# Strassen products over twelve instead of eight k-tiles, with most of the weight sums made by accumulating DMAs

## The chip, the cores and the metric

The kernel runs on one core of a Trainium2 chip. The metric is the device time of one execution in microseconds, the median of several runs. A core has TensorE for matrix products, VectorE (DVE) and ScalarE (ACT) for elementwise work, GpSimd (POOL), SyncE (SP), whose queue here issues the loads, and 16 DMA engines that move data between HBM and the on-chip memory SBUF. TensorE writes its sums into eight PSUM banks.

## The reference

One decoder layer on 256 tokens of width 2048, all in float32:

```python
x = layer_norm(ALPHA * x + 0.5 * swiglu(x, ffn1_w_in[i], ffn1_w_out[i]), ln_g[i, 0], ln_b[i, 0])
z = x @ mix_w_in[i]
...
x = layer_norm(ALPHA * x + merged @ mix_w_out[i], ln_g[i, 1], ln_b[i, 1])
x = layer_norm(ALPHA * x + 0.5 * swiglu(x, ffn2_w_in[i], ffn2_w_out[i]), ln_g[i, 2], ln_b[i, 2])
ple = jax.nn.sigmoid(x @ ple_w_gate[i]) * (p[i] @ ple_w_proj[i])
x = layer_norm(ALPHA * x + ple, ln_g[i, 3], ln_b[i, 3])
```

`swiglu(x, w_in, w_out)` splits `x @ w_in` into halves a and u, each 5504 columns wide, and returns `(silu(a) * u) @ w_out`. The two feed-forward blocks hold most of the arithmetic, and the change is in their first product, `x @ w_in`. The input p is 256 wide and used only in the last product.

## The kernel before

**Three passes for one product.** Every operand is kept as a pair: h, its value rounded to the fast format fp32r, and l, the rest. A product is three matmuls, h x h, h x l and l x h (lines 962 to 964, in `passes`). The 128 x 128 block of tokens is the stationary operand, 512 columns of a weight are the moving one. There are two row blocks of tokens, t = 0 and 1, and a depth of 2048 is 16 k-tiles of 128.

**How a weight comes in.** Weights are handled in elements of two k-tiles x 512 columns, 512 KB. SP loads an element into a raw tile (`weight_dma`, line 868), ScalarE casts it to h (`weight_cast`, line 897), VectorE subtracts to get l (`weight_split`, line 908). The pairs h and l lie in a ring of six ("main", `NMAIN`), with some more in a few regions (`EXTRA`). `feed` runs after each consumed element and issues loads, casts and splits as far as buffers allow; `plan` is the list of all elements in the order in which TensorE uses them, and casts and splits follow it. Instructions of one engine run in the order that this gives.

**Chunks of a feed-forward block.** The 5504 columns of a and of u are cut into 11 chunks of up to 512. Chunks 0 and 1 are plain (`Unit`, one for a and one for u); chunks 2 to 10 are each a `Quad`, which treats the 2 row blocks and the 2 column blocks (a and u) together. After a chunk mostly two output products (`out_unit`) follow, which multiply an earlier chunk pair's result with `w_out`, eight k-tiles deep.

**Strassen in a Quad.** For four k-tiles (two "lo", two "hi"), the four column-block and depth-block parts of the weight are the tiles k11, k12, k21 and k22. Winograd's form of Strassen's method makes seven products instead of eight, into the banks p1 to p7: three elements of loaded tiles (11, 22, 21) and four sums of them (t1 to t4). The sums are made in place: t1 is k11 + k12 in k11's buffer, t3 is k12 + k22 in k12's, t2 adds k22 to k11's buffer, t4 adds k21 to it. Line 891, in `weight_cast`, is that sum on VectorE. The token side has its own sums s1 to s4, made once per block by `sums` from transposed plain copies of x. Two steps cover k-tiles 0 to 7. The other eight are ordinary elements a0, a1 (column block a, used for both row blocks) and u0, u1 (column block u); the Strassen form wants row block 0's u product as the difference d of the row blocks. In each step the order is 11 u0 t1 u1 22 t3 a0 t2 a1 21 t4. An element makes 6 passes, an a or u element 12. At the end of the second step, `after` combines the banks into the four results, applies silu and the product, and `turn` transposes the result three ticks later. A tick is one group of six passes; `defer` runs work a number of ticks later.

**Buffers.** Loaded Strassen tiles lie in a ring of five (`NSRAW`, tag `sraw`), shared with the plain copies of x until `sums` is through at tick 11 of its region; other raw tiles in a ring of four (`NRAW`). `may_load` lets a ring load when a buffer's last reader has been issued.

**The operand p.** `small_loads`, at the start of the program, loads p; `place` transposes it and makes its pair in tiles `ph` and `pl` of the pool `low`, which stay until the last stage.

Of the kernel before, what the change touches and what calls it, by code (L numbers as in the profile page):

```python
# [10 lines left out]
F32 = mybir.dt.float32  # L11
# [6 lines left out]
P = 128  # L18
D = 2048
S = 256  # L20
NT = 2
# [9 lines left out]
LONG = (12, 4)  # L31
EXTRA = {"lead1": 3, "ffn1": 0, "tail1": 4, "hgrn": 0, "merge": 0, "lead2": 3, "ffn2": 0, "tail2": 4, "ple": 1}
NSRAW = 5
# [33 lines left out]
class Quad:  # L67
# [10 lines left out]

    def __init__(self, stat, w, cols, width, after):
        self.stat, self.w, self.cols, self.width, self.after = stat, w, cols, width, after  # L80
        self.els = []
        for s in range(2):
            lo, hi = (2 * s, 2 * s + 1), (4 + 2 * s, 5 + 2 * s)
            n0, n1 = (8 + 4 * s, 9 + 4 * s), (10 + 4 * s, 11 + 4 * s)
            k11, k12, k21, k22 = ((self, s, n) for n in ("11", "12", "21", "22"))
            step = {
                "11": dict(src=k11, use=[("p1", 0, lo)]),
                "t1": dict(src=k11, add=k12, use=[("p5", "s1", lo)]),
                "22": dict(src=k22, use=[("p3", "s4", lo)]),
                "t3": dict(src=k12, add=k22, use=[("p7", "s3", lo)], free=[k12]),  # L90
                "t2": dict(src=k11, add=k22, use=[("p6", "s2", lo)], drop=[k22]),
                "21": dict(src=k21, use=[("p2", 0, hi)]),
                "t4": dict(src=k11, add=k21, use=[("p4", 1, hi)], drop=[k21], free=[k11]),
            }
            for n, ks in (("a0", n0), ("a1", n1)):
                step[n] = dict(load=[(ks, 0)], use=[("p2", 0, ks), ("p4", 1, ks)])
            for n, ks in (("u0", n0), ("u1", n1)):
                step[n] = dict(load=[(ks, 1)], use=[("p3", "d", ks), ("p5", 1, ks)])
            step["11"]["sums"] = [(k12, lo, 1), (k22, hi, 1), (k21, hi, 0), (k11, lo, 0)]
            order = "11 u0 t1 u1 22 t3 a0 t2 a1 21 t4".split()  # L100
            for n in order:
                self.els.append(dict(step[n], name=n, step=s))
# [3 lines left out]
def hybrid_layer(ctx: ExitStack, tc: tile.TileContext, x, p, ln_g, ln_b, ffn1_w_in, ffn1_w_out, mix_w_in,  # L106
# [24 lines left out]
    def open_region(kind):  # L131
# [6 lines left out]
        if kind.startswith("lead"):  # L138
            region["high"] = reopen("hctx", kind + "h", "right")
            held.update(sraw=0, freed=0)  # L140
# [135 lines left out]
    def high(name):  # L276
        held["sraw"] += 1
        return region["high"].tile([P, KG, CC], F32, tag="sraw", name=name, bufs=NSRAW)

    def plain_tile(t, c):  # L280

        if c % 2 == 0:
            plain[t, c // 2] = high("yT")
        return plain[t, c // 2][:, c % 2, :]

    def difference(a, b, o):
        nc.vector.tensor_tensor(out=o, in0=a, in1=b, op=ALU.subtract)

    def sums(stat):
        x1, x2, d = plain[0, 0], plain[1, 0], high("s3")  # L290
        x11, x12, x21, x22, s3 = x1[:, 0, :], x1[:, 1, :], x2[:, 0, :], x2[:, 1, :], d[:, 0, :]
        s1, s2, s4 = x21, x11, x12

        def made(key, g, src):
            halves(stat, key, g, src, 4, "s")

        def third():
            difference(x11, x21, s3)
            made("s3", 0, s3)

        def first():
            difference(x21, x22, s1)
            made("s1", 0, s1)

        def second():
            difference(s1, x11, s2)
            made("s2", 0, s2)

        def fourth():
            nc.vector.tensor_tensor(out=s4, in0=x12, in1=s2, op=ALU.add)  # L310
            made("s4", 0, s4)

        def delta(c):
            a = plain[0, 1][:, c % 2, :]
            difference(a, plain[1, 1][:, c % 2, :], a)
            made("d", c, a)
            if c == 3:
                held["freed"] += 5

        for i, fn in enumerate((third, first, second, fourth, lambda: delta(2), lambda: delta(3))):  # L320
            defer(1 + 2 * i, fn)
# [85 lines left out]
    def ffn(name, xs, w_in, w_out, ln_i, nxt):  # L407
# [7 lines left out]
        def in_units(ch, g, ci):  # L415
            c0 = starts[ch]
            w = starts[ch + 1] - c0
            if ch > 1:
# [8 lines left out]
                def after(el, ps):  # L427
                    if el["step"] == 0:
                        return
                    if el["name"] == "11":  # L430
                        made["c11"] = work("h")
                        nc.scalar.copy(made["c11"], ps["p1"])
                    elif el["name"] == "22":
                        made["c12"] = work("silu")
                        nc.scalar.copy(made["c12"], ps["p3"])
                        both(made["c12"], made["c12"], ps["p5"], ALU.add)
                    elif el["name"] == "t2":
                        made["e"], made["c22"] = work("silu"), work("h")
                        e = made["e"]
                        both(e, made["c11"], ps["p6"], ALU.add)  # L440
                        both(made["c12"], made["c12"], e, ALU.subtract)
                        both(e, e, ps["p7"], ALU.add)
                        both(made["c22"], ps["p5"], e, ALU.subtract)
                    elif el["name"] == "21":
                        h = made["c11"]
                        both(h, h, ps["p2"], ALU.add)
                        nc.scalar.activation(h, h, AF.Silu)
                        both(h, h, made["c12"], ALU.mult)
                        turn(g, 0, ci, h, CC)
                    elif el["name"] == "t4":  # L450
                        e = made["e"]
                        both(e, e, ps["p4"], ALU.add)
                        nc.scalar.activation(e, e, AF.Silu)
                        both(e, e, made["c22"], ALU.mult)
                        turn(g, 1, ci, e, CC)

                units.append(Quad(xs, w_in, (c0, DFF + c0), CC, after))
# [44 lines left out]
        units.append(("tail" + name, lambda: None))  # L502
# [14 lines left out]
    def small_loads():  # L517
# [6 lines left out]
        pin = [st.tile([P, CC], F32, tag="h", name="pin", bufs=3) for t in range(NT)]  # L524
        for t in range(NT):
            nc.sync.dma_start(pin[t][:, :256], p[0, 0, t * P : (t + 1) * P, :])

        def place():
            tp = ptile("t", "tp")
            nc.tensor.transpose(tp[:, :96], gb, ident[:96, :96])  # L530
            nc.vector.tensor_copy(gbT, tp[:, :96])
            for t in range(NT):
                tp = transposed(pin[t], 2)
                ph = low.tile([P, 2, P], F32R, tag=f"ph{t}", name="ph")
                pl = low.tile([P, 2, P], F32R, tag=f"pl{t}", name="pl")
                hf = ph.rearrange("p a b -> p (a b)")
                nc.scalar.copy(hf, tp[:, :256])
                nc.vector.tensor_tensor(out=pl.rearrange("p a b -> p (a b)"), in0=tp[:, :256],
                                        in1=hf.bitcast(F32), op=ALU.subtract)
                pst.parts[t, 0] = (ph, pl)  # L540

        defer(8, place)

# [255 lines left out]
    pst = Stat()  # L799
# [33 lines left out]
    loads = {"raw": deque(), "sraw": deque()}  # L833
    for u in units:
# [3 lines left out]
        if isinstance(u, Quad):  # L838
            for el in u.els:
                for key, ks, n in el.get("sums", ()):  # L840
                    loads["sraw"].append((key, kind, u.w, ks[0] * P, 2, u.cols[n], u.width))
                if "load" in el:
                    (ks, n), = el["load"]
                    el["src"] = len(plan)
                    el["free"] = [len(plan)]
                    loads["raw"].append((len(plan), kind, u.w, ks[0] * P, 2, u.cols[n], u.width))
                plan.append(dict(el, n=2, w=u.width, where="main"))
            continue
# [8 lines left out]
    used = {"raw": 0, "sraw": 0}  # L857
    room = dict(EXTRA, main=NMAIN)

    def weight_dma(ring="raw"):  # L860
# [4 lines left out]
        else:  # L865
            raw = high("sraw")
# [4 lines left out]
    def may_load(ring):  # L871
# [4 lines left out]
        return loads[ring][0][1] == region["kind"] and 5 <= held["freed"] and held["sraw"] - held["freed"] < NSRAW  # L876

    def drop(keys):
        for key in keys:
# [3 lines left out]
            else:  # L883
                held["freed"] += 1

    def weight_cast():
# [3 lines left out]
        if "add" in el:  # L890
            nc.vector.tensor_tensor(out=raw[:, :n, :w], in0=raw[:, :n, :w], in1=raws[el["add"]][:, :n, :w], op=ALU.add)  # L891
            drop(el.get("drop", ()))
# [19 lines left out]
    def castable():  # L912
# [135 lines left out]
```

## Time and profile before

| | us |
|---|---|
| median of three runs | 2227.79 (2227.02 to 2231.14) |
| the profiled execution | 2228.56 |
| its span, first to last instruction | 2226.7 |

In the profile, "busy" is the time in which an engine executed something; matmuls overlap, so TensorE's busy share says that it was never without one, not how fast it was. L963 is line 963. "bank<-wl,xh" is what is written from what is read, by the program's names. The feed-forward blocks lie at about 20 to 710 us and 1430 to 2130 us of the span.

### The profile page before, as it was taken

To read this page: it belongs to the slowest core of one execution; us is meant where nothing else is said; L and a number is where in the kernel's file an instruction comes from. 1 tells how busy PE (TensorE), PEld (TensorE's weight loads), DVE (VectorE), ACT (ScalarE), POOL (GpSimd) and SP (SyncE) were. 2 spreads that over 40 slices of the span, in tenths; PEclk is the share of its full clock that TensorE was granted. 3 is DMA by queue.
4 is the path that set the end of the run, shared out by engine and by line. 5 is a ranking of instruction groups with operands and counts; after the bars stand their busy time and mean duration, and the time that the engine had idled before them with its cause. 6 is when DMAs were issued, how large, how long until landed. Compare 5 with 4: busy or idle time off the path is not lost.

```text
span 2226.7 us, 26935 instructions
## 1 busy us (share of the span) xinstructions
PE 2203.0 (99%) x10110; PEld 1837.0 (82%) x10110; DVE 1685.6 (76%) x1952; ACT 1127.8 (51%) x1324; POOL 10.0 (0%) x32
## 2 busy tenths in 40 slices
PE   9999999999999999999999999999999999999997
PEld 7988888888887888888888888798888888888876
DVE  6788888888885678557555875769888888888668
ACT  5555555555555534434444443645555555555463
POOL 1000000000000000000000000000000000000000
PEclk9999999999999999999999999999999999999999
DMA  7666676566653665554555665567666556666564
GB/s 255 215 204 194 198 217 202 183 192 190 207 194 128 194 200 172 174 167 152 189 190 189 199 194 192 181 200 226 209 214 197 181 185 214 200 191 192 172 218 151
DMA packets 225334, 429.98 MB, mean 193 GB/s; under 512 B 13740, under 2 KB 22452, under 8 KB 225204
## 3 DMA queue, kind: packets, MB, share of 16 engines
q1 hardware_dynamic: 225204, 428.27, 60.6%
q8 instruction: 79, 1.29, 0.2%
q14 instruction: 51, 0.42, 0.1%
HBM read 426.12 MB, written 2.10 MB: 192 GB/s over the span
## 4 chain that ended last, share of the span: by engine, by line
PE 92%; DVE 4%; DMA 2%; ACT 1%; issue 1%; SPq 0%; DVEq 0%; ACTq 0%
PE bank L962 30%; PE bank L964 29%; PE bank L963 29%; DVE wl L908 2%; PE bank L243 2%; PE bank L600 1%; DVE sraw L891 1%; DMA raw<-in_ffn_w_in_dram 1%; ACT wh L897 0%; DMA sraw<-in_ffn_w_in_dram 0%; DMA gb<-in_ln_g_dram 0%; DMA x<-in_x_dram 0%; DMA raw<-in_ffn_w_out_dram 0%; DVE x L400 0%; DVE x L401 0%
## 5 line engine op out<-in xcount | busy, mean ns | idle before, releaser
L908 DVE TENSOR_TENSOR wl<-raw,wh 128x1024 fp32r<-128x1024 f32 (+2 forms) x660 | 788.6, 1203 | 262.8 <-ACT wh L897 245.4
L897 ACT CAST wh<-raw 128x1024 fp32r<-128x1024 f32 (+2 forms) x660 | 680.4, 1035 | 581.5 <-PE bank L964 410.1
L964 PE MATMUL bank<-wh,xl 128*128 128x512 f32 (+1 forms) x1736 | 670.9, 387 | 0.7 <-DVE xl L254 0.7
L963 PE MATMUL bank<-wl,xh 128*128 128x512 f32 (+1 forms) x1736 | 671.0, 387 | 0.0
L962 PE MATMUL bank<-wh,xh 128*128 128x512 f32 (+1 forms) x1736 | 669.6, 388 | 1.3 <-ACT xh L253 0.9
L897 ACT CAST wh<-sraw 128x1024 fp32r<-128x1024 f32 x252 | 262.5, 1050 | 273.1 <-PE bank L964 120.3
L908 DVE TENSOR_TENSOR wl<-sraw,wh 128x1024 fp32r<-128x1024 f32 x252 | 306.1, 1223 | 102.5 <-ACT wh L897 98.8
L964 PEld LDWEIGHTS bank<-wh,xl 128*128 128x128 f32 x1736 | 327.0, 188 | 64.5 <-DVE xl L254 2.4
L962 PEld LDWEIGHTS bank<-wh,xh 128*128 128x128 f32 x1736 | 327.1, 188 | 63.9 <-ACT xh L253 1.7
L963 PEld LDWEIGHTS bank<-wl,xh 128*128 128x128 f32 x1736 | 327.0, 188 | 61.8 <-DVE wl L908 0.2
L963 PE MATMUL bank<-wl,gh 128*128 128x512 f32 x880 | 343.9, 391 | 0.0
L964 PE MATMUL bank<-wh,gl 128*128 128x512 f32 x880 | 342.9, 391 | 0.0
L962 PE MATMUL bank<-wh,gh 128*128 128x512 f32 x880 | 341.9, 392 | 0.0
L964 PEld LDWEIGHTS bank<-wh,gl 128*128 128x128 f32 x880 | 165.4, 188 | 34.1
L962 PEld LDWEIGHTS bank<-wh,gh 128*128 128x128 f32 x880 | 165.3, 188 | 33.8
L963 PEld LDWEIGHTS bank<-wl,gh 128*128 128x128 f32 x880 | 165.4, 188 | 33.4
L891 DVE TENSOR_TENSOR sraw<-sraw 128x1024 f32<-128x1024 f32 x144 | 175.8, 1221 | 0.7
L964 PE MATMUL bank<-wh,sl 128*128 128x512 f32 x432 | 168.5, 390 | 0.0
L963 PE MATMUL bank<-wl,sh 128*128 128x512 f32 x432 | 168.4, 390 | 0.0
L962 PE MATMUL bank<-wh,sh 128*128 128x512 f32 x432 | 164.9, 390 | 0.5 <-ACT wh L897 0.5
L962 PEld LDWEIGHTS bank<-wh,sh 128*128 128x128 f32 x432 | 81.1, 188 | 17.9 <-ACT wh L897 1.4
L963 PEld LDWEIGHTS bank<-wl,sh 128*128 128x128 f32 x432 | 81.1, 188 | 16.9
(181 smaller groups left out, 1145.8 us busy)
## 6 DMA issues: line engine op xcount, KB each, us to landing
raw<-in_ffn_w_in_dram SPq DMA_DIRECT2D x176, 512.0 KB, 4.5
raw<-in_mix_w_in_dram SPq DMA_DIRECT2D x176, 512.0 KB, 4.6
raw<-in_ffn_w_out_dram SPq DMA_DIRECT2D x168, 512.0 KB, 4.9
sraw<-in_ffn_w_in_dram SPq DMA_DIRECT2D x144, 512.0 KB, 4.7
raw<-in_mix_w_out_dram SPq DMA_DIRECT2D x32, 512.0 KB, 5.4
raw<-in_ple_w_gate_dram SPq DMA_DIRECT2D x32, 512.0 KB, 4.9
raw<-in_ffn_w_in_dram SPq DMA_DIRECT2D x32, 384.0 KB, 4.0
raw<-in_branch_w_conv_dram SPq DMA_DIRECT2D x16, 512.0 KB, 4.9
```

The lines of the kernel that those rows point to most:

```text
L243: state["turned"] = nc.tensor.transpose(tp[:, i * P : (i + 1) * P], src[:, i * P : (i + 1) * P], ident).ins
L600: nc.tensor.matmul(gp[:, (h * 2 + t) * 64 : (h * 2 + t + 1) * 64], kd[:, h, t * P : (t + 1) * P], qd[:, h, t, :], start=True, stop=True)
L891: nc.vector.tensor_tensor(out=raw[:, :n, :w], in0=raw[:, :n, :w], in1=raws[el["add"]][:, :n, :w], op=ALU.add)
L897: nc.scalar.copy(h[:, :n, :w], raw[:, :n, :w])
L908: nc.vector.tensor_tensor(out=l[:, :n, :w], in0=raw[:, :n, :w], in1=h[:, :n, :w].bitcast(F32), op=ALU.subtract)
L962: nc.tensor.matmul(acc, sh, wh[:, a, :n], start=first, stop=False)
L963: nc.tensor.matmul(acc, sh, wl[:, a, :n], start=False, stop=False)
L964: nc.tensor.matmul(acc, sl, wh[:, a, :n], start=False, stop=last)
```

## The change

- A Quad makes three Strassen steps (`STEPS`), over twelve k-tiles, and has two a and two u elements left. One order for the whole Quad, `ORDER`, interleaves the steps: the next step's first elements stand between the last ones of the step before.
- Of the twelve weight sums of a Quad, the eight in `BY_DMA` are made by a DMA that GpSimd's queue issues with an adding write (`accum_op=ALU.add`); t1.0, t1.1, t1.2 and t4.2 stay on VectorE. The sums leave `weight_cast` and get a function of their own, `weight_add`. A sum is issued, in the plan's order, when both tiles have been asked for and the splits in `behind` have been issued.
- The ring of five becomes rings by part (`HIGH`): two tiles for 11, one each for 12, 21 and 22. A load into them is asked for ahead of ordinary loads.
- `after` becomes a list of (banks, function): each runs, in order, when its banks have got their last product.
- The token side needs sums for six k-tiles instead of four, and d for four instead of eight; `sums` makes them in ten deferred parts up to tick 19, after which the rings are open. Its pairs' ring has 7 buffers instead of 6.
- p is loaded and made into a pair at the start of the second block's tail, in buffers that the feed-forward results use, instead of at the start.

```diff
+HIGH = {"11": 2, "12": 1, "21": 1, "22": 1}
...
+    STEPS = (((0, 1), (4, 5)), ((2, 3), (6, 7)), ((8, 9), (10, 11)))
+    ORDER = ("11.0 22.0 t1.0 u0 21.0 t3.0 t2.0 11.1 u1 t4.0 22.1 t1.1 a0 21.1 t3.1 t2.1 "
+             "11.2 a1 t4.1 22.2 t1.2 t3.2 21.2 t2.2 t4.2").split()
+    BY_DMA = "t3.0 t2.0 t4.0 t3.1 t2.1 t4.1 t3.2 t2.2".split()
...
+                "11": dict(src=k11, use=[("p1", 0, lo)], load=[(k11, lo, 0), (k22, hi, 1), (k12, lo, 1), (k21, hi, 0)]),
+                "t1": dict(src=k11, add=k12, behind="11", use=[("p5", "s1", sums)]),
+                "22": dict(src=k22, use=[("p3", "s4", sums)]),
+                "t3": dict(src=k12, add=k22, behind="t1", use=[("p7", "s3", sums)], free=[k12]),
+                "t2": dict(src=k11, add=k22, behind="t1 22", use=[("p6", "s2", sums)], drop=[k22]),
                 "21": dict(src=k21, use=[("p2", 0, hi)]),
-                "t4": dict(src=k11, add=k21, use=[("p4", 1, hi)], drop=[k21], free=[k11]),
+                "t4": dict(src=k11, add=k21, behind="t2 21", use=[("p4", 1, hi)], drop=[k21], free=[k11]),
...
-            order = "11 u0 t1 u1 22 t3 a0 t2 a1 21 t4".split()
...
-        where, bufs = {"m": (region["pool"], 4), "s": (region["pool"], 6)}.get(tag, (op, 8))
+        where, bufs = {"m": (region["pool"], 4), "s": (region["pool"], 7)}.get(tag, (op, 8))
...
+        todo = (low_sums, lambda: made("s1", x[2]), lambda: made("s2", x[0]), lambda: made("s3", s3),
+                lambda: made("s4", x[1]), high_sums, lambda: made_two(one, "s1", "s2"),
+                lambda: made_two(two, "s3", "s4"), delta, lambda: held.update(on=True))
+        for i, fn in enumerate(todo):
             defer(1 + 2 * i, fn)
...
+                after = deque([(("p1",), first), (("p3", "p5"), second), (("p6", "p7"), third),
+                               (("p2",), fourth), (("p4",), fifth)])
...
-        units.append(("tail" + name, lambda: None))
+        units.append(("tail" + name, p_operand if ln_i else lambda: None))
...
+    def p_operand():
+        for t in range(NT):
+            pin = st.tile([P, CC], F32, tag="h", name="pin", bufs=3)
+            nc.sync.dma_start(pin[:, :256], p[0, 0, t * P : (t + 1) * P, :])
+            defer(8 + t, lambda t=t, pin=pin: to_stat(pst, t, 0, pin, 2, "g"))
...
+    def weight_add():
+
+        el = plan[adds.popleft()]
+        a, b = raws[el["src"]], raws[el["add"]]
+        if el["by_dma"]:
+            nc.gpsimd.dma_start(a, b, accum_op=ALU.add)
+        else:
+            nc.vector.tensor_tensor(out=a, in0=a, in1=b, op=ALU.add)
+        drop(el.get("drop", ()))
+        el["added"] = True
+
+    def addable():
+        if not adds:
+            return False
+        i = adds[0]
+        el = plan[i]
+        if el["src"] not in raws or el["add"] not in raws or cur["split"] <= el["behind"]:
+            return False
+        return el["by_dma"] or i <= cur["split"] + 1
...
-        if "add" in el:
-            nc.vector.tensor_tensor(out=raw[:, :n, :w], in0=raw[:, :n, :w], in1=raws[el["add"]][:, :n, :w], op=ALU.add)
-            drop(el.get("drop", ()))
...
-        return (el["src"] in raws and el.get("add", el["src"]) in raws and room[el["where"]]
+        return (el["src"] in raws and ("add" not in el or el.get("added")) and room[el["where"]]
...
-            if may_load("sraw"):
-                weight_dma("sraw")
-            elif may_load("raw"):
-                weight_dma()
+            ring = next((r for r in ("11", "22", "12", "21", "raw") if may_load(r)), None)
+            if ring:
+                weight_dma(ring)
+            elif addable():
+                weight_add()
...
-            u.after(el, ps)
+            while u.after and all(b in left and not left[b] for b in u.after[0][0]):
+                u.after.popleft()[1](ps)
```

More of the change, by code (lines that the diff above doesn't have):

```diff
@@ L94, in __init__ @@
             }
[L95 to L99, printed above, removed]
-            order = "11 u0 t1 u1 22 t3 a0 t2 a1 21 t4".split()
-            for n in order:
-                self.els.append(dict(step[n], name=n, step=s))
+            for n, el in step.items():
+                name = f"{n}.{s}"
+                if "behind" in el:
+                    el["behind"] = max(self.ORDER.index(f"{m}.{s}") for m in el["behind"].split())
+                    el["by_dma"] = name in self.BY_DMA
+                made[name] = el
@@ L289, in sums @@
     def sums(stat):
[L290 to L320, printed above, removed]
+        def both(o, a, b, op):
+            nc.vector.tensor_tensor(out=o, in0=a, in1=b, op=op)
@@ new lines, in four, with low_sums @@
+        def four(x11, x12, x21, x22, s1, s2, s3, s4):
+            both(s3, x11, x21, ALU.subtract)
+            both(s1, x21, x22, ALU.subtract)
+            both(s2, s1, x11, ALU.subtract)
+            both(s4, x12, s2, ALU.add)
+        lo, hi, spare = [plain[t, 0] for t in range(NT)], [plain[t, 1] for t in range(NT)], high("11", "s")
+        x = [lo[0][:, 0, :], lo[0][:, 1, :], lo[1][:, 0, :], lo[1][:, 1, :]]
+        s3 = spare[:, 0, :]
+        def low_sums():
+            four(*x, x[2], x[0], s3, x[1])
@@ new lines, in made, with high_sums, made_two @@
+        def made(n, src):
+            halves(stat, n, 0, src, 4, "s")
+        one, two = lo[1][:, 1, :], spare[:, 1, :]
+        def high_sums():
+            h = P * 2
+            y = [hi[t][:, 0, i * h : (i + 1) * h] for t in range(NT) for i in range(2)]
+            four(*y, one[:, :h], one[:, h:], two[:, :h], two[:, h:])
+        def made_two(src, a, b):
+            halves(stat, a + b, 0, src, 4, "s")
+            h, l = stat.parts[a + b, 0]
+            stat.parts[a, 1], stat.parts[b, 1] = (h[:, 0:2, :], l[:, 0:2, :]), (h[:, 2:4, :], l[:, 2:4, :])
@@ L425, in both @@
                     nc.vector.tensor_tensor(out=o, in0=a, in1=b, op=op)
[L427 to L455, printed above, removed]
@@ L531, in place @@
             nc.vector.tensor_copy(gbT, tp[:, :96])
[L532 to L540, printed above, removed]
-        defer(8, place)
+        defer(8, place)
+    pst = Stat()
+    def p_operand():
[3 more added lines that the diff above has]
+            defer(8 + t, lambda t=t, pin=pin: to_stat(pst, t, 0, pin, 2, "g"))
     def small_inputs():
@@ L832, in hybrid_layer @@
     plan = []
-    loads = {"raw": deque(), "sraw": deque()}
+    adds = deque()
+    loads = {ring: deque() for ring in ("raw", *HIGH)}
     for u in units:
@@ L838, in hybrid_layer @@
         if isinstance(u, Quad):
+            base = len(plan)
             for el in u.els:
[L840 to L846, printed above, removed]
+                if "add" in el:
+                    adds.append(len(plan))
+                    el["behind"] += base
+                for key, ks, n in el.get("load", ()):
+                    ring = key[2] if key else "raw"
+                    if not key:
+                        key = el["src"] = len(plan)
+                        el["free"] = [key]
+                    loads[ring].append((key, kind, u.w, ks[0] * P, 2, u.cols[n], u.width))
                 plan.append(dict(el, n=2, w=u.width, where="main"))
@@ L856, in hybrid_layer @@
     cur = {"cast": 0, "split": 0}
-    used = {"raw": 0, "sraw": 0}
+    used = {"raw": 0}
     room = dict(EXTRA, main=NMAIN)
@@ L865, in weight_dma @@
         else:
-            raw = high("sraw")
+            raw = high(ring, "raw" + ring)
+            held[ring] += 1
         src = w[r0 : r0 + n * P, col : col + width].rearrange("(a p) c -> p a c", p=P)
@@ L875, in may_load @@
             return used["raw"] < NRAW
-        return loads[ring][0][1] == region["kind"] and 5 <= held["freed"] and held["sraw"] - held["freed"] < NSRAW
+        return loads[ring][0][1] == region["kind"] and held["on"] and held[ring] < HIGH[ring]
     def drop(keys):
```

64 lines of the change are left out of this document (42 added, 22 removed).

## The prediction

> **What bounds the kernel now.** I read the page's header and busy line first, then TensorE's own waits, then windows over the feed-forward stages, then the groups by form inside one of these windows, and the DMA views last.
>
> ```profile
> span 2226.7 us, 26935 instructions
> PE 2203.0 (99%) x10110; PEld 1837.0 (82%) x10110; DVE 1685.6 (76%) x1952; ACT 1127.8 (51%) x1324; POOL 10.0 (0%) x32
> PEclk9999999999999999999999999999999999999999
> ...
> PE bank L962 <- ACT wh L897: 0.5, 2, 0.3
> ...
> 160.00:640.00 480.00, 480.00 (x2145) 397.50 (x2144) 407.19 (x403) 259.38 (x276) 0.00 (x0) 1.00 0.63 196
> 1520.00:2080.00 560.00, 559.49 (x2500) 462.60 (x2499) 480.21 (x485) 303.54 (x325) 0.00 (x0) 1.00 0.64 202
> ```
>
> The windows' columns are start:end, length, then busy time and count of PE, weight load, VectorE, ScalarE and GpSimd, the granted clock, the DMA share and GB/s. TensorE is busy for all of 480 us in the first feed-forward block and misses 0.5 us of 560 in the second, where twice it waits for the cast of a weight pair. The clock is full. So only fewer or shorter matmuls can make these stages faster, and everything else counts only if it becomes late. VectorE is next at 407 of 480 us, 85%; the DMA engines are at 0.63, ScalarE at 54%, GpSimd idle.
>
> ```profile
> 1060.00:1220.00 160.00, 91.22 (x236) 44.14 (x235) 1.00 0.60 195
> ```
>
> This row counts only L963, one of the three passes of each product, in a stretch of pure matmul. 160 us / (3 x 236) = 0.226 us per 128x512 pass.
>
> **What the change takes from TensorE.** A chunk of 512 feed-forward columns (a Quad) covers 16 k-tiles, 2 row blocks and 2 column blocks. Four ordinary k-tiles of one step take 16 products; Strassen takes seven products of two k-tiles, 14. Before: 2 steps x 14 + 8 k-tiles x 4 = 60 products, 180 passes. After: 3 x 14 + 4 x 4 = 58 products, 174 passes. There are nine such chunks in each block, 18 in all: 18 x 6 = 108 passes x 0.226 = **24.4 us** off an engine with no slack. The 16 loads of 512 KB a chunk stay.
>
> **What it asks of VectorE and ScalarE.**
>
> ```profile
> L908 DVE TENSOR_TENSOR wl<-sraw,wh 128x1024 fp32r<-128x1024 f32 x108 | 131.3, 1223 | 47.9 <-ACT wh L897 46.1
> L897 ACT CAST wh<-sraw 128x1024 fp32r<-128x1024 f32 x107 | 111.4, 1050 | 112.1 <-PE bank L964 47.2 <-DMA sraw<-in_ffn_w_in_dram 35.5 <-DVE sraw L891 27.9
> L891 DVE TENSOR_TENSOR sraw<-sraw 128x1024 f32<-128x1024 f32 x61 | 74.4, 1220 | 0.3
> ```
>
> A weight element (two k-tiles of one column block) needs a cast, 1.05 us, and a split, 1.22 us; a weight sum adds 1.22 us. Elements per chunk go from 2 x 7 + 8 = 22 to 3 x 7 + 4 = 25. Sums go from 8 to 12, of which 8 leave VectorE. VectorE per chunk: +3 splits - 4 sums = -1 x 1.22 us, 22 us less in all; ScalarE +3 x 1.05 us, 57 us more in all, on an engine that is about half free. Both lie beside TensorE, so they are costed at nothing; VectorE's load per TensorE time stays as it was (30 big operations per 180 passes before, 29 per 174 after). Without that relief, four more sums a chunk (4.9 us) would push VectorE over.
>
> **The sums by DMA.** Eight times a chunk, 144 in all, GpSimd's queue issues a transfer that adds one 512 KB tile into another. GpSimd is at 0.00 in both windows, so nothing queues behind these issues but the next sums. The trace has no such transfer, so its time X, from its operands being ready to its landing, must be bounded:
>
> ```profile
> DMA to landing us min/median/max: 3.6/4.6/6.2
> ...
> out_dram<-x SPq DMA_DIRECT2D x8, 256.0 KB, 2.3
> ```
>
> The first row is the load of an equal tile from HBM in the window of the first block, the second a store of half the size. Lower end 2.3 us; upper end twice the median load, 9.2 us, since a sum reads two tiles. I take **3.8 us**: it is nearest to the shortest loads, since it moves as many bytes to the same place but leaves HBM out.
>
> The Trainium skill, "DMA: Bandwidth & Descriptors", section "Anatomy of one DMA — SWDGE (gpsimd) path", fits such a transfer by about 2.0 us plus its bytes over 436 GB/s; no run here shows it, and with the two reads counted the estimate is 4.4 us.
>
> What X may be follows from the order. The six main weight pairs are the lookahead: element i can be cast only when TensorE has finished element i-6. TensorE takes 6 passes, 1.36 us, on an element and twice that on a0, a1, u0, u1. In the new order t1.1 stands at place 11; its pair comes free when place 5 is done, 7 units or 9.5 us after the chunk's first pass; its split ends 1.05 + 1.22 = 2.27 us later, at 11.8 us. The last element, t4.2, is wanted 28 units in, at 38.0 us. Between lies the longest chain, since k11's buffer is summed in place again and again and the casts go in order: t2.1's sum (X), cast and split; t4.1's sum (X), cast and split; t1.2's VectorE sum, cast and split; t2.2's sum (X), cast and split; t4.2's VectorE sum, cast and split. That is 3X + 5 x 2.27 + 2 x 1.22 = 3X + 13.8 us against 26.2 us: **X up to 4.1 us costs nothing**. Above, each microsecond costs up to 3 us a chunk, 54 us in all. The gain of 1.36 us a chunk is gone at X = 4.6 us. At 3.8 us the chain fits with 1.0 us to spare. The first two steps have more room: before t2.0 stand long elements of the output product, and u1 and a1 stand ahead of t4.0 and t4.1.
>
> What is queued behind a late sum: on ScalarE the next casts, on VectorE the splits behind them; on SP, the load into a buffer that the sum reads (k22, k21), and behind it the ordinary loads.
>
> **The smaller edits, together.**
>
> ```profile
> 58.00 3.98 SPq L868 DMA_DIRECT2D sraw<-in_ffn_w_in_dram  x4
> 83.10 1.05 ACT L897 CAST wh<-sraw 128x1024 fp32r<-128x1024 f32 x1 [0.20 <-PE bank L964]
> 40.92 0.42 DVE L538 TENSOR_TENSOR pl<-bank,ph 128x256 fp32r<-128x256 f32 x1
> 40.00:60.00 20.00, 20.00 (x95) 16.77 (x94) 12.06 (x17) 10.03 (x16) 0.00 (x0) 1.00 0.64 199
> 2080.00:2100.00 20.00, 20.00 (x90) 16.58 (x89) 9.22 (x10) 4.20 (x4) 0.00 (x0) 1.00 0.51 163
> ```
>
> The operand sums now end at tick 19 instead of 11, and only then may the first chunk's tiles be loaded: 8 ticks x 1.36 = 11 us later. Before, 25 us lie between these loads and the first cast of one, so 14 us are left, three loads' time. One more operand half and some subtractions join VectorE there, beside the second plain chunk; nothing. The split of p leaves the first 46 us, where TensorE is full anyway (third and fourth row), so nothing is won, and goes to the tail of the second block, where VectorE is under half busy and ScalarE at a fifth (last row). Its two loads join SP's queue and may hold it until a tile of the last chunk is turned, some 4 us by three ticks; the ordinary raw tiles and ten weight pairs cover that, at 2.7 us of TensorE each. With that cover gone it would cost those 4 us once.
>
> **The sum.** The profiled execution took 2228.56 us, its span 2226.7; the median shown is 2227.79, 0.8 us less. 2228.6 - 24.4 = 2204.2; from the median 2203.4. With a microsecond or so for the start of a block, I say **2205 us**. Below that little can lie: TensorE's stalls in the two windows sum to 0.5 us.
>
> **The rivals.**
>
> *Slower: the sums come late.* This is the chain above with another X. For it speaks that the load's median is 4.6 us, just the point where the gain is gone, and that the sums share the engines with loads. Against it, that no HBM is in them and that 3.6 us occurs. At X = 5 us: 18 x 3 x 0.4 = +22, 2250 us; at 6.2 us, the slowest load, 18 x 3 x 1.6 = +86, 2314 us. It decides from 4.6 us on.
>
> *Part of the gain, or nothing, is left.* X between 4.1 and 4.6 us gives 2204 to 2228; it has the same reasons for and against, with a smaller miss.
>
> The skill's fit named above falls here: at its 4.4 us the chain would give back 18 x 3 x 0.27 = 15 us, 2219 us.
>
> *Slower: the DMA engines become the bound.*
>
> ```profile
> q1 hardware_dynamic: 48767, 93.96, 62.5%
> ```
>
> In the 480 us of the first block, 62.5% x 480 = 300 us of all 16 engines carried 93.96 MB, 179 loads' worth: 1.67 us for each 512 KB. A chunk with its two output products has 24 such loads, 40.2 us, in 276 x 0.226 = 62.4 us before and 61.0 after. Eight sums at one load each make 53.6 us, which fits; at two loads each, for two reads, 67.0 us, which doesn't: 4.6 us longer than before, 18 x 4.6 = +83, 2311 us. It binds from 20.8 / 8 = 2.6 us a sum and loses from 22.2 / 8 = 2.8. Against it: packet time that contains HBM's latency overstates what the engines are taken up with.
>
> That a sum reads twice is a rule of the Trainium skill, "Collectives: The Full Stack", section "The bandwidth ceiling: the fold count and why AG ≠ RS ≠ AR": a reducing transfer sends two reads through the ring for each write, and ran at half a copy's rate. No run here shows it yet; by it this rival would hold if the 1.67 us were all occupancy.
>
> *The change doesn't do what it says*, so that TensorE issues as many passes as now: the count above speaks against it, and I give it nothing of its own.
>
> **How the numbers follow.** Forecast, with X under 4.1 us (2201 to 2210): 0.53. Part of the gain (2210 to 2223): 0.08. Within 0.2%, about what a measurement of this kernel can tell from no change, 2223 to 2232: 0.10. Late sums: 0.21. DMA-bound: 0.08. Faster 0.61, same 0.10, slower 0.29. The range goes from 2200 to 2265: X up to 5.3 us is within it, half of the slower cases lie above, about 0.15, and little lies below. The forecast's own range is 2201 to 2210.
>
> **What would show it.** Right: 108 passes fewer on L962 to L964's counterparts, TensorE full in both blocks, VectorE's share of these stretches as now, and casts that wait for sums no longer in all than they wait for loads now. Wrong, by the chain: TensorE idle some microseconds near the end of each chunk, released by the cast of t4 and behind it a DMA sum over 4.6 us. Wrong, by capacity: a DMA share over 0.95 and loads that land much later than 4.6 us. My forecast falls with X; if X is small and TensorE still stalls, the order of the casts is what I misread.

## The result, and the profile after

The changed kernel is **slower**: 2412.55 us, the median of four runs (2403.37 to 2414.68), against 2228.51 us for the kernel before on the same chip. The ratio is 1.0817, with a 95% interval from 1.0786 to 1.0847. The profiled run took 2413.95 us. The repeated executions of each kernel below lie within 0.5% of each other, but for one of the four with only the t3 sums by DMA, which took 3148.68 us at a granted clock of 0.652 and is left out.

These are rows of the page of the kernel after: header, busy time, the two large queues (packets, MB, share of 16 engines) and the landing of the new transfers.

```profile
span 2412.2 us, 27290 instructions
...
PE 2266.2 (94%) x10002; PEld 1830.8 (76%) x10002; DVE 1668.3 (69%) x1942; ACT 1167.0 (48%) x1380; POOL 132.4 (5%) x176
...
q1 hardware_dynamic: 225204, 428.27, 54.4%
q0 software_dynamic: 20736, 75.51, 18.1%
...
raw<-raw POOLq DMA_DIRECT2D x144, 512.0 KB, 5.7
```

TensorE issues 10002 matmuls instead of 10110: the 108 passes are gone. Yet it is without a matmul for 2412.2 - 2266.2 = 146.0 us, where it was 23.7 us before. The sums land in 5.7 us at the median, not in 3.8. The windows of the two blocks, in the same stretches as before:

```profile
160.00:640.00 480.00, 437.43 (x1818) 340.36 (x1817) 339.77 (x336) 234.58 (x255) 46.69 (x55) 0.97 0.86 231
1520.00:2080.00 560.00, 510.29 (x2157) 403.13 (x2156) 392.37 (x402) 273.31 (x305) 47.53 (x56) 0.97 0.84 227
```

TensorE, full before, misses 43 and 50 us here, and its clock falls to 0.97. No other engine has become the bound: VectorE fell from 407 to 340 us and ScalarE from 259 to 235, mainly because less work gets through. The DMA share rose from 0.63 to 0.86. What they waited for, from the view of waits (engine, line and tile, releaser: total, times, longest):

```profile
ACT wh L932 <- DMA raw<-raw: 356.2, 115, 7.0
...
ACT wh L932 <- DMA raw<-in_ffn_w_out_dram: 111.9, 72, 9.2
...
PE bank L998 <- ACT wh L932: 81.6, 101, 3.3
...
PE bank L999 <- DVE wl L943: 40.0, 59, 0.9
```

Read from the bottom: TensorE waits 121.6 us for splits and casts; the casts (L932) wait 356 us for the transfers that write a raw tile from a raw tile, the sums. The tile view of those transfers gives their spread:

```profile
DMA to landing us min/median/max: 4.5/5.7/9.0
```

**One chunk, followed through.** First GpSimd's timeline (start, duration, line, [idle before <- releaser]). The eight rows of a chunk are, in order, the sums t3.0, t2.0, t4.0, t3.1, t2.1, t4.1, t3.2 and t2.2; the last row here is the next chunk's t3.0.

```profile
448.15 0.84 POOL L909 DMA_DIRECT2D raw<-raw  x1 [30.04 <-DVE raw L911]
450.34 0.86 POOL L909 DMA_DIRECT2D raw<-raw  x1 [1.34 <-DVE wl L943]
459.36 0.84 POOL L909 DMA_DIRECT2D raw<-raw  x1 [8.17 <-DVE wl L943]
463.76 0.86 POOL L909 DMA_DIRECT2D raw<-raw  x1 [3.55 <-DVE raw L911]
469.49 0.84 POOL L909 DMA_DIRECT2D raw<-raw  x1 [4.87 <-DVE wl L943]
478.95 0.86 POOL L909 DMA_DIRECT2D raw<-raw  x1 [8.62 <-DVE wl L943]
483.10 0.84 POOL L909 DMA_DIRECT2D raw<-raw  x1 [3.29 <-DVE raw L911]
488.82 0.85 POOL L909 DMA_DIRECT2D raw<-raw  x1 [4.88 <-DVE wl L943]
520.43 0.84 POOL L909 DMA_DIRECT2D raw<-raw  x1 [30.75 <-DVE raw L911]
```

Then the casts on ScalarE, each row one cast or several back to back, from the start of the first:

```profile
456.76 2.95 ACT L932 CAST wh<-raw 128x1024 fp32r<-128x1024 f32 x3 [2.93 <-DMA raw<-raw]
464.62 3.90 ACT L932 CAST wh<-raw 128x1024 fp32r<-128x1024 f32 x4 [4.91 <-PE bank L1000]
...
476.35 2.94 ACT L932 CAST wh<-raw 128x1024 fp32r<-128x1024 f32 x3 [3.35 <-DMA raw<-raw]
483.95 2.94 ACT L932 CAST wh<-raw 128x1024 fp32r<-128x1024 f32 x3 [4.67 <-DMA raw<-raw]
...
493.99 1.05 ACT L932 CAST wh<-raw 128x1024 fp32r<-128x1024 f32 x1 [2.50 <-DMA raw<-raw]
```

And TensorE: the chunk's first pass, then the first pass of its last element t4.2.

```profile
452.10 0.40 PE L998 MATMUL bank<-wh,xh 128*128 128x512 f32 x1
...
498.74 0.49 PE L998 MATMUL bank<-wh,xh 128*128 128x512 f32 x1 [0.98 <-ACT wh L932]
```

Put together, the five sums into k11's two buffers run strictly one after another. From issue to the cast of the sum: t2.0 450.34 to 456.76, t4.0 459.36 to 464.62, t2.1 469.49 to 476.35, t4.1 478.95 to 483.95, t2.2 488.82 to 493.99. That is 6.42 + 5.26 + 6.86 + 5.00 + 5.17 = 28.7 us, a mean X of 5.74. (The second row names TensorE as the releaser; the time fits the landing as well.) The stretches between a cast and the next issue, in which casts, splits and VectorE's own sum run, add up to 14.9 us, and 4.75 us lie between the last of these casts and t4.2's pass: 5X + 19.7 = 48.4 us from t2.0's issue. TensorE wanted t4.2 28 units (six passes, 1.356 us) after 452.10, at 490.1; it got it at 498.74, 8.6 us late. From t3.0 to the next t3.0 the chunk takes 72.3 us, where its 270 passes alone would take 61.0. It is a typical one: from the first chunk's t3.0 at 86.52 to the ninth's at 668.38 the mean period is 72.7 us, and in the run without these sums (below) it is 61.5, by t1.0 from 84.18 to 576.22. Eighteen times 11.2 us is 202 us, nearly all of the 209 that were lost against that run.

### The profile page after: what moved, and what is told of

It reads as the page before. It is cut to its first block, busy times and chain, and to the rows that moved or that the text cites. A ratio compares the mean times of both kernels' runs of the same rounds, so it can differ in the third digit from the quotient of the medians.

```text
span 2412.2 us, 27290 instructions
## 1 busy us (share of the span) xinstructions
PE 2266.2 (94%) x10002; PEld 1830.8 (76%) x10002; DVE 1668.3 (69%) x1942; ACT 1167.0 (48%) x1380; POOL 132.4 (5%) x176
## 3 DMA queue, kind: packets, MB, share of 16 engines
q1 hardware_dynamic: 225204, 428.27, 54.4%
q0 software_dynamic: 20736, 75.51, 18.1%
## 5 line engine op out<-in xcount | busy, mean ns | idle before, releaser
L943 DVE TENSOR_TENSOR wl<-raw,wh 128x1024 fp32r<-128x1024 f32 (+2 forms) x966 | 1142.0, 1209 | 552.4 <-ACT wh L932 537.8
L932 ACT CAST wh<-raw 128x1024 fp32r<-128x1024 f32 (+2 forms) x966 | 972.2, 1038 | 1056.4 <-PE bank L1000 374.2
L998 PE MATMUL bank<-wh,xh 128*128 128x512 f32 (+1 forms) x1628 | 641.5, 397 | 39.6 <-ACT wh L932 36.9
L999 PE MATMUL bank<-wl,xh 128*128 128x512 f32 (+1 forms) x1628 | 639.8, 394 | 13.4 <-DVE wl L943 13.3
L1000 PE MATMUL bank<-wh,xl 128*128 128x512 f32 (+1 forms) x1628 | 635.1, 391 | 0.3 <-DVE xl L263 0.3
L998 PE MATMUL bank<-wh,sh 128*128 128x512 f32 x504 | 205.9, 410 | 36.5 <-ACT wh L932 36.1
L999 PE MATMUL bank<-wl,sh 128*128 128x512 f32 x504 | 207.6, 412 | 24.2 <-DVE wl L943 24.1
L909 POOL DMA_DIRECT2D raw<-raw x144 | 122.4, 850 | 1727.4 <-DVE raw L911 707.7
L1000 PE MATMUL bank<-wh,sl 128*128 128x512 f32 x504 | 202.2, 401 | 0.0
L1000 PEld LDWEIGHTS bank<-wh,sl 128*128 128x128 f32 x504 | 98.2, 195 | 19.2
L911 DVE TENSOR_TENSOR raw<-raw,raw 128x1024 f32<-128x1024 f32 x72 | 88.1, 1224 | 26.1 <-DMA raw<-in_ffn_w_in_dram 25.6
```

The source lines that it names most:

```text
L909: nc.gpsimd.dma_start(a, b, accum_op=ALU.add)
L911: nc.vector.tensor_tensor(out=a, in0=a, in1=b, op=ALU.add)
L932: nc.scalar.copy(h[:, :n, :w], raw[:, :n, :w])
L943: nc.vector.tensor_tensor(out=l[:, :n, :w], in0=raw[:, :n, :w], in1=h[:, :n, :w].bitcast(F32), op=ALU.subtract)
L998: nc.tensor.matmul(acc, sh, wh[:, a, :n], start=first, stop=False)
L999: nc.tensor.matmul(acc, sh, wl[:, a, :n], start=False, stop=False)
```

## The experiments

Each time is compared with the kernel before on the same chip (medians 2227.1 to 2228.8) and, as "over e1", with the first experiment's 2203.52 us. Where no interval is given there was one run, and only differences of tens of microseconds are read. Where a text names no other place, the edit is in `weight_add`, whose line was `nc.gpsimd.dma_start(a, b, accum_op=ALU.add)`.

### Everything but the DMA sums

```diff
-            nc.gpsimd.dma_start(a, b, accum_op=ALU.add)
+            pass
```

> The eight sums a chunk that the DMA engines make are left out (the output is not the reference's); the four on VectorE, the order, the rings and all loads stay. Every theory that blames the sums by DMA (late landing, DMA capacity, SP held up by loads that wait for sums) expects TensorE full in both blocks and 2204 us, within 6. If the order, the smaller rings or the late p cost something by themselves, it stays above 2215.

2203.52 us, 23.6 less than before. The busy line of the page and the window of the first block:

```profile
PE 2177.6 (99%) x10002; PEld 1816.2 (82%) x10002; DVE 1669.3 (76%) x1942; ACT 1184.2 (54%) x1380; POOL 9.7 (0%) x32
```

```profile
160.00:640.00 480.00, 479.48 (x2142) 396.15 (x2141) 408.02 (x412) 291.51 (x308) 0.00 (x0) 1.00 0.62 201
```

TensorE is full again. So the fewer passes are worth what was reckoned, and the new order, the rings by part, the later operand sums and the late p together cost at most about a microsecond, as far as one run can tell. All of the 209 us comes with the eight sums.

### Their waits, without their bytes

```diff
+            nc.gpsimd.dma_start(a[:, :1, :16], b[:, :1, :16], accum_op=ALU.add)
```

> Each DMA sum adds only 16 columns of one k-tile, 8 KB instead of 512 KB (the rest of the sum is left out): the same transfers, waits and queue, no bytes. Landing should fall to some 2 to 3 us. Late landing: below the chain's 4.1 us, so 2204 us, within 8. Capacity: the same. If the issue on GpSimd's queue or the wait for a semaphore as such were the cost, well above 2250.

> Each sum is two 8 KB sums one behind the other (the rest of the sum is left out): about 2 x 2.3 us and a little, some 4.9 us from issue to the last landing, hardly any bytes. With one small sum (2.7 us to landing) the time was 2214 us, with three 2682 us. Late landing alone sets the time: between the plain copy's 2289 us at 4.4 us and the changed kernel's 2412 us at 5.7 us, so 2300 to 2360 us. Capacity sets much of those two: well below 2289 us.

> Each sum is three 8 KB sums on the same bytes one behind the other (the rest of the sum is left out): about three times the small transfer's time to landing, 6 to 9 us, as late as the real sum's 5.7 us or later, with hardly any bytes. Late landing as the cause: 2400 us or more. DMA capacity as the cause: about 2210 us. In between, both count, and the share says how much.

The edit is e3's; e9 and e4 issue it two and three times in series, so that each waits for the landing of the one before. One small sum: 2213.68 us, 10 over e1, landing in 2.0/2.7/5.9 us (min/median/max). SP's queue is then held for 334 us by loads that wait for sums, about as long as in the kernel after, so that wait as such is cheap; so is GpSimd's issue (0.85 us each). Two in series: 2437.52 us, 234 over e1. Three: 2681.72 us, 478 over e1. The rows of the run with two, from its page and from the first block's window:

```profile
q0 software_dynamic: 41472, 2.38, 3.0%
```

```profile
160.00:640.00 480.00, 433.81 (x1807) 339.71 (x1805) 337.49 (x335) 232.66 (x253) 93.44 (x110) 0.97 0.58 170
```

Compare this window with the one of the kernel after: TensorE 434 against 437 us, VectorE 337 against 340, ScalarE 233 against 235, the same clock, but a DMA share of 0.58 against 0.86. These are, in one chunk, the first issues of t2.0, t4.0, t2.1, t4.1 and t2.2 on GpSimd, and the casts of these sums on ScalarE:

```profile
382.92 0.84 POOL L910 DMA_DIRECT2D raw<-raw  x1 [0.35 <-DVE wl L944]
390.54 0.84 POOL L910 DMA_DIRECT2D raw<-raw  x1 [4.50 <-DVE wl L944]
401.30 0.84 POOL L910 DMA_DIRECT2D raw<-raw  x1 [3.64 <-DVE wl L944]
410.09 0.84 POOL L910 DMA_DIRECT2D raw<-raw  x1 [5.68 <-DVE wl L944]
420.77 0.84 POOL L910 DMA_DIRECT2D raw<-raw  x1 [3.66 <-DVE wl L944]
...
387.93 2.94 ACT L933 CAST wh<-raw 128x1024 fp32r<-128x1024 f32 x3 [2.49 <-DMA raw<-raw]
396.43 5.79 ACT L933 CAST wh<-raw 128x1024 fp32r<-128x1024 f32 x6 [5.55 <-DMA raw<-raw]
407.49 2.94 ACT L933 CAST wh<-raw 128x1024 fp32r<-128x1024 f32 x3 [5.28 <-PE bank L1001]
415.91 2.94 ACT L933 CAST wh<-raw 128x1024 fp32r<-128x1024 f32 x3 [5.47 <-DMA raw<-raw]
425.71 1.04 ACT L933 CAST wh<-raw 128x1024 fp32r<-128x1024 f32 x1 [3.59 <-DMA raw<-raw]
```

From issue to cast the five take 5.0, 5.9, 6.2, 5.8 and 4.9 us, 27.8 in all where the kernel after has 28.7, and the chunk takes 71.7 us against 72.3. So **a delay of this length costs the whole loss with hardly a byte moved**. A little of the delay is not landing: GpSimd's queue waits for the first half of t3.0 too, so t2.0 is issued 3.5 us behind t3.0 here (379.42 to 382.92) and 2.2 us in the kernel after. The expectation had too small a slope.

### Their bytes, with less waiting

```diff
+            nc.gpsimd.dma_start(a, b)
```

> The transfer copies the second tile over the first instead of adding it (the sums are left out): the same bytes written, one read instead of two, same queue. Capacity with two reads: 144 transfers fall from 18.1% of the 16 engines' time to about 9 to 10%, and the time to below 2260 us. Late landing: time to landing falls to about 4.6 us, and by the chain 2204 + 18 x 3 x 0.5 = 2231 us. If reading twice doesn't matter: 2412 us as with the sum.

A plain copy instead of the sum: 2289.19 us, 86 over e1. From the page:

```profile
q0 software_dynamic: 20736, 75.51, 8.4%
...
raw<-raw POOLq DMA_DIRECT2D x144, 512.0 KB, 4.4
```

The same 75.51 MB written, but 8.4% of 2287.5 us over 144 is 1.33 us of the 16 engines for each, where a sum takes 18.1% of 2412.2, 3.03 us. It lands 1.3 us earlier and 123 us of the loss go with that. But for 4.4 us the predicted chain gives 15 us and the recounted one below (4.4 - 4.0) x 90 = 36, and 86 were measured.

To load the engines without a wait, three runs put other transfers in place of a sum:

> In place of each sum (left out) two 512 KB copies from x to the output array, both in HBM, that nobody waits for (the output is written over at the end): at 1.6 us each about the sum's 3.0 us of all 16 engines, so the same load on the DMA engines with no chain. Late landing as the cause: TensorE stays full, 2204 to 2225 us, the loads only land later. Capacity as the cause: 2300 us or more.

> As the dead copies, but each pair of 512 KB copies in HBM now waits, like the sum that it stands for, for the split ahead of it (GpSimd reads 8 columns of that split first), so that the load on the DMA engines comes when the sums' does, about 2.7 us of all 16 engines each, and nobody waits for it; the sums are left out. Capacity by itself: 2300 us or more. Late landing: 2204 to 2230 us, since only the loads land later.

> Each DMA sum is replaced (the sums are left out) by two stores of its second tile, 512 KB each, to the output array, which is written over at the end: the same queue, time of issue and hold on the second tile's buffer, 2.7 us of all 16 engines or so, but no cast waits for it. Capacity, or SP held by buffers that the sums keep, as a cause of its own: 2260 us or more. Only the wait of the casts for a late landing: 2204 to 2235 us.

The first two came to 2595.42 and 2516.24 us and **say nothing**: their copies ran ahead of the kernel, all 288 of e10 within the first 560 us (DMA share 0.99 there), and those of both blocks in e11 within 950 us. The third writes the tile that a sum would read to the output, twice 512 KB, so it can't run ahead of its load: 2275.61 us, 72 over e1. The transfers take 17.3% of 2273.9 us, 2.73 us for each pair, near a sum's 3.03. Of its waits, one row stands out:

```profile
DVE raw L914 <- DMA raw<-in_ffn_w_in_dram: 106.5, 35, 5.5
```

VectorE's sum waits for loads, 36.9 us in e1. So bytes that keep the engines and the raw buffers busy cost something by themselves. The stores also go to HBM, which sums don't, so 72 us is not the sums' own share.

### Which sums

> The five DMA sums into k11's buffer (t2.0, t4.0, t2.1, t4.1, t2.2) stay, the three t3 sums are left out. In the changed kernel these five are issued one behind the other's split, so if they carry the loss: 2340 to 2400 us. If the loss grows with the number of sums alone: 2204 + 5/8 x 209 = 2335 us. If the chain is not what counts: below 2300 us.

> The three t3 sums by DMA stay, the five into k11's buffer are left out. With all of those on VectorE the time was 2296 us, with every sum on VectorE 2273. If only the k11 chain counts: 2204 to 2215 us. If each landing counts where the casts, in order, meet it: some 2 us a sum, 18 x 3 x 1.5 or so, 2260 to 2300 us.

e17 keeps the five sums into k11 (t2 and t4), e18 the three into k12 (t3); the other sums by DMA are not made. e17: 2384.49 us, **181 over e1**. e18: 2310.09 us, 107 over e1. Together 288 where both cost 209: they overlap. Rows of the waits of e17, then of e18:

```profile
ACT wh L933 <- DMA raw<-raw: 383.0, 85, 6.3
```

```profile
ACT wh L933 <- DMA raw<-raw: 160.4, 47, 6.1
...
DVE raw L912 <- DMA raw<-in_ffn_w_in_dram: 101.8, 33, 5.1
```

The five sums into k11 alone are enough for most of the loss. The t3 sums, which the prediction gave no part, hold the casts too, and VectorE's sum waits for its load. That k12's single buffer, which a late t3 frees later, is the reason follows from the program and isn't shown by itself.

### Fewer sums by DMA, or none

```diff
-    BY_DMA = "t3.0 t2.0 t4.0 t3.1 t2.1 t4.1 t3.2 t2.2".split()
+    BY_DMA = ()
```

> All twelve sums on VectorE, the rest of the change as it is. VectorE per chunk: 33 splits and 12 sums at 1.14 us back to back and about 9 us of shorter work, 60 us of TensorE's 61. Late landing as the cause of the loss: no sum takes longer than 1.2 us, so most of the loss goes, 2215 to 2260 us, what is left being VectorE. Below 2204 it can't go.

> t3.0, t2.0, t3.1 and t2.1 by DMA, eight sums on VectorE: as many as in the run with the t3 sums and t2.0, but two of them in k11's chain. Late landing: slower than that run by about one landing's lateness a chunk, 10 to 40 us. VectorE alone as the cause: the same time as that run.

> Only the three t3 sums of a chunk by DMA, the other nine on VectorE. The t3 sums stand outside the chain through k11's buffer. Late landing along k11's chain (t2.0, t4.0, t2.1, t4.1, t2.2, five sums in series): the chain is free of DMAs, and VectorE has 3.4 us less a chunk than with all twelve, so below 2273 us, 2205 to 2240. If any sum by DMA costs its landing time, 2273 us or more.

> The three t3 sums and t2.0 by DMA, eight on VectorE, so that VectorE has as many large operations a chunk as before the change or less. One DMA sum of the chain, with the output products' long elements ahead of it: if that place has the room that the prediction gave it, about as the run with the t3 sums alone or some 20 us less; if not, slower than that by up to 18 x 2 us.

| sums by DMA | us | ratio to before (95%) |
|---|---|---|
| none (e2, one run) | 2273.30 | 1.020 |
| t3.0 t3.1 t3.2 (e12) | 2295.87 | 1.0299 (1.0281 to 1.0318) |
| these and t2.0 (e13) | 2326.64 | 1.0441 (1.0419 to 1.0463) |
| t3.0 t2.0 t3.1 t2.1 (e8) | 2349.57 | 1.0543 (1.0524 to 1.0561) |
| eight (the change) | 2412.55 | 1.0817 (1.0786 to 1.0847) |

The more sums by DMA, the slower. By the prediction's chain t3 by DMA should have beaten all on VectorE, and t2.0 should have been free: neither held. With none, VectorE is the bound, in bursts rather than on the average; window and wait of e2:

```profile
160.00:640.00 480.00, 466.35 (x2049) 379.00 (x2048) 452.40 (x444) 271.38 (x288) 0.00 (x0) 1.00 0.60 193
```

```profile
PE bank L999 <- DVE wl L943: 30.9, 39, 1.2
```

VectorE works 452 of 480 us here, and TensorE waits for splits. So the premise that VectorE could not carry all sums was right; it costs 70 us over e1.

Two more runs issue a sum as early as its operands allow, t3 ahead of t1's split, with t3 by DMA (e15) or with none (e16):

> As the run with only the t3 sums by DMA (2296 us), but each sum on VectorE is issued as soon as its tiles are free, and each t3 sum right behind t1's, some seven elements or 11 us ahead of its cast instead of one to three. Late landing: a sum of 6.5 us is then covered and VectorE has nine sums instead of twelve, 2204 to 2235 us. If DMA sums cost by their mere number (capacity, GpSimd's queue): 2290 us as before.

> All twelve sums on VectorE, issued as soon as their tiles are free: tells what the earlier issue does without a DMA. VectorE has as much to do as with all sums on it in the old place (2273 us): 2255 to 2275 us. The difference to the run with t3 sums by DMA is what three covered DMA sums a chunk save.

e15: 2293.66 us, 1.0299 (1.0282 to 1.0316), hardly better than e12. In the chunk from 411 us the casts of t3.0, t3.1 and t3.2 come 4.6, 7.5 and 7.0 us after the issue, and ScalarE sits idle before each, so the landing isn't covered. Why t3 isn't issued earlier isn't shown. VectorE's sums wait for their loads only 1.2 us in all there, which speaks against the single k12 tile as the whole reason; another is that the sums keep one order, so that t3.1 stands behind t4.0 in `adds`. e16: 2267.61 us, 1.0181 (1.0166 to 1.0196), the best with twelve Strassen k-tiles, and slower than before.

### The sums on GpSimd

```diff
+            nc.gpsimd.tensor_tensor(out=a, in0=a, in1=b, op=ALU.add)
```

> The eight sums as elementwise additions on GpSimd instead of DMAs. GpSimd copies 128x1024 in 1.17 us, so a sum of two tiles should take 2 to 3 us, less than the 4.1 us that the chain allows: 2204 to 2215 us by late landing, if GpSimd and VectorE don't get in each other's way. If they do, sums take 4 us or more, or VectorE's 1.22 us operations get longer, and the time is above 2228 us.

2371.88 us. The groups by form in 360 to 640 us (count | busy, mean ns | idle before):

```profile
L943 DVE TENSOR_TENSOR wl<-raw,wh 128x1024 fp32r<-128x1024 f32 x131 | 218.0, 1712 | 12.6 <-ACT wh L932 12.5
...
L909 POOL TENSOR_TENSOR raw<-raw,raw 128x1024 f32<-128x1024 f32 x32 | 98.6, 3082 | 184.5 <-DVE raw L911 124.6 <-DVE wl L943 59.8
```

GpSimd needs 3.1 us for a sum, and meanwhile VectorE's split grows from 1.22 to 1.71 us at the mean, with hardly any idle time left before it (12.6 us for 131 splits). Over the run TensorE waits 95.0 us for splits and 29.9 for casts. The Trainium skill, "SBUF — State Buffer", section "Who interferes with whom", says that a VectorE instruction with two SBUF inputs contends with a GpSimd instruction that reads SBUF, and that DMAs contend with no engine. This run agrees with the first, and the kernel after with the second: its splits in the first block's window still take 1.222 us.

## Why the prediction was wrong

**TensorE's term was right.** 24.4 us for 108 passes; e1 measured 23.6, at 2203.52 us close to the forecast of 2205. The relief of VectorE was needed (e2), and the smaller edits cost about a microsecond at most (e1).

**The step that failed is the chain: "3X + 13.8 us against 26.2 us: X up to 4.1 us costs nothing", with X at 3.8 us.** Two things were wrong in it.

*X.* The nearest row was taken to be the shortest load, because a sum leaves HBM out. It lands in 4.5 us at best and 5.7 at the median, later than a load of the same size (4.6), so it lies beyond the limit throughout. Twice the load, the upper end, was too high, but the reason for it, that a sum reads two tiles, is what the 3.03 us against a copy's 1.33 fit.

*How often X is paid.* "The first two steps have more room" was an assertion without a sum. In the trace t2.0 and t4.0 wait as t2.1, t4.1 and t2.2 do, since the casts run in order and each sum waits for a split behind the sum before. So t2.1 is issued at 469.49, 17.4 us after the chunk's first pass, where the prediction let its chain begin at 11.8. With five in series the chain is 5X + 19.7, and from t2.0's issue to t4.2's due time lie 490.1 - 450.34 = 39.8 us: the limit is X = 4.0 us, nearly as predicted, but each microsecond above costs 5 a chunk, 90 in all, not 54. (5.74 - 4.0) x 90 = 157 us. e9 shows such a delay at work without the bytes, e17 these five sums without the others.

**The same 209 us, read on TensorE**, are what a broken stream costs. Its idle time grew by 146.0 - 24.2 = 122 us against e1, its busy time by 2266.2 - 2177.6 = 89 us for the same passes. The granted clock, 0.978 over the run against 0.996, accounts for an estimated 2177.6 x (0.996/0.978 - 1) = 40 us of the second. After most waits a pass stands alone for 0.50 us where the next follows after 0.227 in a stream: 160 waits x 0.27 = 44 us. The prediction had no term for the clock or the lone passes. The 157 us of the chain are a part of this loss and not added to it; of the other 52 it isn't shown what they are, but the t3 sums, which the chain leaves out, cost 107 alone (e18).

**The rival of late sums was the right mechanism at too low a price**: its 54 us for each microsecond would have given 2204 + 1.6 x 54 = 2290 at the measured X. The range, which went up to X = 5.3 us, ended 148 us short.

**The DMA rival decided at 2.6 us a sum, and a sum took 3.03.** With a load's 54.4% x 2412.2 / 817 = 1.61 us (428.27 MB are 817 loads' worth), 24 loads and eight sums are 62.9 us of the 16 engines in a chunk that should take 61.0. So by that count it would have failed there too, by 1.9 us a chunk or 34 us; e14, with no sum to wait for, lost 72. But it isn't what sets the time after: the share is 0.86, and e9 is as slow at 0.58. The engine time of a sum is 3.03 / 1.33 = 2.3 times a copy's. The prediction cited from the Trainium skill, "Collectives: The Full Stack", section "The bandwidth ceiling: the fold count and why AG ≠ RS ≠ AR", that a reducing transfer reads twice and runs at half a copy's rate. The trace agrees and goes somewhat beyond.

**SP held by loads that wait for sums** was named as a danger and is none: 342 us of such waits after, 334 in e3, which lost 10.

**What stays open.** How much of the real sum's loss is waiting and how much is bytes that occupy engines and buffers: the waiting alone is enough (e9), e5 lost 86 us at a landing for which the recounted chain gives 36, and e14 lost 72 with no wait for a sum. Also whether a second k12 tile, or sums issued out of order, would let t3 land unseen; neither was tried.

## What to carry to other kernels

Before work moves from an engine to a transfer, follow the chain it joins through the whole period and count how often the landing is paid in series: here five times a chunk, through a buffer summed in place and casts in a fixed order. Moving busy time off an engine is no gain if its 1.2 us become 5.7 us of latency ahead of something that TensorE needs. Where the landing time is unknown and the slack is a fraction of a microsecond, price the miss by that count, and add what restarts, and perhaps a lower clock, cost once TensorE's stream breaks.

## What the runs showed of the hardware

- An adding DMA of 512 KB from SBUF to SBUF takes 3.03 us of the 16 engines and lands in 5.7 us beside loads; a plain copy 1.33 us and 4.4. With 8 KB it still lands in 2.0 us at best and 2.7 at the median.
- GpSimd is busy 0.85 us for the issue of an adding transfer, 0.53 for a copy.
- In runs whose stream on TensorE the DMA sums broke, the granted clock was lower: 0.996 in e1, 0.978 in the kernel after, 0.928 in e4. Idle time alone doesn't set it: in e7 TensorE is without a matmul for 148 us, as long as in the kernel after (146), and the clock is 0.996.
